# Three modulation blocks move from the first FFN's f tiles into the first mixer of a two-layer trunk

## The chip, the cores and the metric

The kernel runs on one core of one Trainium2 chip. The metric is device time in microseconds (us), the median of several executions. Each profile is of one execution.

## What is computed

The reference is a two-layer decoder trunk over 256 tokens of width 1024, in float32. Every sub-layer normalises, scales and shifts by a vector made from the conditioning row `c`, and adds its gated output:

```python
c_act = silu(c)
for i in range(2):
    mod = c_act @ mod_w[i] + mod_b[i]                 # 9 vectors of 1024
    sh1, sc1, g1, sh2, sc2, g2, sh3, sc3, g3 = split(mod, 9)
    h = rmsnorm(x, norm_g[i, 0]) * (1 + sc1) + sh1
    x = x + 0.5 * g1 * swiglu(h, w13[i, 0], w2[i, 0])          # d_ff 2816
    h = rmsnorm(x, norm_g[i, 1]) * (1 + sc2) + sh2
    x = x + g2 * (pool_ssd_mixer(h) if i == 0 else mla_mixer(h))
    h = rmsnorm(x, norm_g[i, 2]) * (1 + sc3) + sh3
    x = x + 0.5 * g3 * swiglu(h, w13[i, 1], w2[i, 1])
return rmsnorm(x, final_norm_g)
```

## The kernel before

**The weights' stream.** Every weight matrix is cut into blocks of 128 x 2048 float32 (1 MB), and the blocks stand in one hand-written list, `items`. SP issues their transfers in that order into six `raw` buffers. A block of kind "w" is worked off in two halves of eight 128x128 tiles ("pieces"): ScalarE (ACT) copies the half to `wh` (L207), VectorE (DVE) writes what is left to `wl` (L213), and TensorE (PE) multiplies with both, since each product is made of a high and a low part. `take()` hands the pieces to PE and keeps four of them made ahead (`LOOK`); five `wh` and `wl` buffers stand behind that.

**Modulation.** The vectors `mod` are not made on PE. A block of kind "m" holds 256 columns of `mod_w`; each of its two halves is one DVE instruction, which multiplies 128x1024 weights by the broadcast `c_bc` and sums along the row into `modc` (L236), with a short read of the accumulator behind it. It is tied to come after the DVE instruction emitted just before it:

```python
prior = last_vector()
V.scalar_tensor_tensor(out=sl, in0=sl, scalar=1.0, in1=c_bc, op0=ALU.mult,
                       op1=ALU.mult, accum_out=modc[:, c0 : c0 + 1])
tc.add_manual_dep(last_vector(), prior.name, ORDER, reason="program order")
```

**Where the blocks of modulation go.** 64 blocks "m" are dealt out between the weight blocks. `phase(blocks, n_mods, skip)` spreads `n_mods` of them evenly behind the weight blocks of one stage, and `MODS` has the number for each stage, in this order: first FFN w13, first FFN w2 (the f tiles), first mixer input (10 blocks), first mixer output projection (4 of its 6 blocks), second FFN w13 and w2, third FFN w13 and w2, second mixer's input and query stages, last FFN:

```python
for i, (ap, n) in enumerate(blocks):
    items.append(("w", ap, n))
    while mods and done * (len(blocks) - skip) < (i + 1 - skip) * n_mods:
        done += 1
        items.append(mods.pop(0))
```

The order of the vectors is fixed: gate 1, scale 2, shift 2, gate 2, scale 3, shift 3, four blocks each, then those of later sub-layers.

**The stages around the change.** In an FFN, `ffn` makes 22 tiles of a and b, then eight f tiles d = 0 to 7, each of 22 pairs of matmuls (L286 with `wh` on the high and low part of `g`, L287 with `wl`); 11 blocks of w2 carry them. Behind each f tile come two residual updates (`xt`, L466), and the next norm's `chunk` (ACT L395 and squares, DVE L396 and L403). `mixer_ab` opens with tiles named B, C and xs on the un-normalised input (`norm.open`, L280 to L282), then makes z and xs tiles (`lin`), convolutions (L681), the products cb, the pooling input u (in four parts), then eight pairs of heads (`heads`, `ymm`), gates and group norms (L852 to L868), and the output projection o: six tiles are kept open and their k range is cut at 4, 8 and 12 (`CUT_A`, `OPEN_A`), then d = 6 and 7 come whole (`rest`). The next FFN opens behind it with tiles u_a and u_b. The order of instructions on each engine is made by a scheduler from the program order and from what is ready; an engine runs its own instructions in that fixed order.

Of the kernel before, what the change touches and what calls it, by code (L numbers as in the profile page):

```python
# [35 lines left out]
U_DVE = 1  # L36
SKIP = 6
SKIP0 = 3
MODS = (10, 11, 3, 0, 8, 8, 8, 8, 3, 1, 4)
NQ = 3  # L40
CUT_M, OPEN_M = (4, 6, 8), 3

# [19 lines left out]
def trunk(ctx, tc, xT, c_row, colsh, pos, kc, cols, rows, mod_w, w13s, w13c, w13, w2, win_a, wdt,  # L62
# [41 lines left out]
    def phase(blocks, n_mods, skip=0):  # L104
        done = 0
# [6 lines that stand above are left out]
    def ffn_items(i, n13, n2):  # L112
        phase([(w13[i * NJ + j - NS], 16) for j in range(NS if i == 0 else 0, NJ)], n13, SKIP if i else SKIP0)
        phase([(w2[i, j], 16) for j in range(11)], n2)

    ffn_items(0, *MODS[0:2])
    phase([(win_a[b], 16) for b in range(U_END)], MODS[2])
    items.append(("f", pool_w, 13))
    phase([(win_a[b], 16) for b in range(U_END, 12)], 0)
    phase([(wout_a[b], 16) for b in range(1)], 0)  # L120
    phase([(wout_a[b], 16) for b in range(1, 5)], MODS[3])
    phase([(wout_a[5], 16)], 0)
    ffn_items(1, *MODS[4:6])
    ffn_items(2, *MODS[6:8])
    phase([(win_m[b], 16) for b in range(4)], MODS[8])
    phase([(wkv[:, 0 : 16 * P], 16), (wkv[:, 16 * P :], 8)], 0)
# [1249 lines left out]
```

## Time and profile before

| what | value |
|---|---|
| median of 3 runs | 1020.24 us (1019.9 to 1023.21) |
| the profiled execution | 1020.18 us |
| its span, first to last instruction | 1018.4 us |
| PE, DVE, ACT busy | 99%, 87%, 61% |
| bytes read from memory | 252.81 MB, 249 GB/s over the span |

The span is what the rows count from; the 1.8 us around it belong to the launch. A busy PE is not PE at its peak, because matmuls are pipelined, so what tells is where PE is idle and who ended it.

### The profile page before, as it was taken

To read this page: it belongs to the slowest core of one execution; us is meant where nothing else is said; L and a number is where in the kernel's file an instruction comes from. 1 tells how busy PE (TensorE), PEld (TensorE's weight loads), DVE (VectorE), ACT (ScalarE), POOL (GpSimd) and SP (SyncE) were. 2 spreads that over 40 slices of the span, in tenths; PEclk is the share of its full clock that TensorE was granted. 3 is DMA by queue.
4 is the path that set the end of the run, shared out by engine and by line. 5 is a ranking of instruction groups with operands and counts; after the bars stand their busy time and mean duration, and the time that the engine had idled before them with its cause. 6 is when DMAs were issued, how large, how long until landed. Compare 5 with 4: busy or idle time off the path is not lost.

```text
span 1018.4 us, 16658 instructions
## 1 busy us (share of the span) xinstructions
PE 1003.1 (99%) x6300; PEld 891.2 (88%) x6300; DVE 885.9 (87%) x1649; ACT 622.0 (61%) x1141; POOL 0.2 (0%) x4
## 2 busy tenths in 40 slices
PE   9999999999999999999999999999999999999997
PEld 7998888889878988888898888889998898888886
DVE  6999998998999898989979988999998789877663
ACT  4685553458896676555447666555688666666542
POOL 0000000000000000000000000000000000000000
PEclk9999999999999999999999999999999999999999
DMA  9988989976644478889875887898743246766501
GB/s 351 414 340 314 353 311 345 347 268 239 251 166 166 130 254 283 291 292 338 301 261 173 314 294 258 298 339 313 269 162 130 83 166 212 272 223 245 180 28 41
DMA packets 39649, 254.94 MB, mean 250 GB/s; under 512 B 4481, under 2 KB 7057, under 8 KB 10514
## 3 DMA queue, kind: packets, MB, share of 16 engines
q1 hardware_dynamic: 39570, 253.89, 68.9%
q8 instruction: 49, 0.80, 0.3%
q14 instruction: 30, 0.25, 0.1%
HBM read 252.81 MB, written 1.06 MB: 249 GB/s over the span
## 4 chain that ended last, share of the span: by engine, by line
PE 92%; DVE 6%; ACT 1%; issue 0%; DVEq 0%; ACTq 0%
PE f L286 14%; PE a L286 13%; PE b L286 13%; PE f L287 7%; PE a L287 7%; PE b L287 7%; PE n L543 4%; PE o L286 4%; DVE raw L236 2%; DVE wl L213 2%; PE o L287 2%; PE s L1107 1%; PE u_a L281 1%; PE u_a L280 1%; PE u_b L281 1%; PE u_b L280 1%
## 5 line engine op out<-in xcount | busy, mean ns | idle before, releaser
L207 ACT CAST wh<-raw 128x1024 fp32r<-128x1024 f32 x327 | 341.1, 1050 | 239.2 <-PE f L286 69.0
L213 DVE TENSOR_TENSOR wl<-raw,wh 128x1024 fp32r<-128x1024 f32 x327 | 396.6, 1218 | 63.7 <-ACT wh L207 63.1
L286 PE MATMUL f<-g,wh 128*128 128x512 f32 x704 | 244.5, 393 | 0.0
L286 PE MATMUL a<-hx,wh 128*128 128x512 f32 x568 | 201.9, 394 | 0.0
L286 PE MATMUL b<-hx,wh 128*128 128x512 f32 x568 | 201.8, 394 | 0.0
L287 PE MATMUL f<-g,wl 128*128 128x256 f32 x704 | 195.4, 279 | 3.3 <-DVE wl L213 3.3
L236 DVE SCALAR_TENSOR_TENSOR raw<-raw,c_bc 128x1024 f32<-128x1024 f32 x144 | 170.7, 1216 | 0.2 <-DMA raw<-in_mod_w 0.2
L287 PE MATMUL a<-hx,wl 128*128 128x256 f32 x568 | 158.3, 279 | 0.0
L287 PE MATMUL b<-hx,wl 128*128 128x256 f32 x568 | 158.3, 279 | 0.0
L286 PEld LDWEIGHTS f<-g,wh 128*128 128x128 f32 x704 | 131.5, 187 | 29.5
L287 PEld LDWEIGHTS f<-g,wl 128*128 128x128 f32 x704 | 132.5, 188 | 4.9 <-DVE wl L213 4.4
L286 PEld LDWEIGHTS b<-hx,wh 128*128 128x128 f32 x568 | 106.5, 187 | 24.5
L286 PEld LDWEIGHTS a<-hx,wh 128*128 128x128 f32 x568 | 106.5, 187 | 24.5 <-DVE hx L421 0.3
L287 PEld LDWEIGHTS a<-hx,wl 128*128 128x128 f32 x568 | 107.0, 188 | 0.4
L287 PEld LDWEIGHTS b<-hx,wl 128*128 128x128 f32 x568 | 107.0, 188 | 0.4
L334 ACT CAST g<-g 128x256 fp32r<-128x256 f32 x88 | 35.2, 403 | 24.9 <-DVE g L617 18.7
L395 ACT ACTIVATE uh<-xt,gs_t 128x256 fp32r<-128x256 f32 x40 | 20.3, 508 | 44.6 <-DVE xt L466 44.5
L286 PE MATMUL o<-hx,wh 128*128 128x512 f32 x128 | 45.8, 401 | 0.0
L466 DVE SCALAR_TENSOR_TENSOR xt<-f,gt_t,xt 128x256 f32<-128x256 f32 x64 | 30.7, 479 | 15.1 <-PE f L287 14.7
L543 PE MATMUL n<-hx,wh 128*128 128x256 f32 x224 | 40.3, 283 | 0.0
L335 DVE TENSOR_TENSOR g<-g,g 128x256 fp32r<-128x256 f32 x88 | 36.6, 419 | 3.9 <-ACT g L334 3.7
L614 ACT COPY tb<-b 128x256 f32<-128x256 f32 x71 | 26.1, 368 | 18.2 <-PE b L287 18.0
(399 smaller groups left out, 1685.5 us busy)
## 6 DMA issues: line engine op xcount, KB each, us to landing
raw<-in_w SPq DMA_DIRECT2D x124, 1024.0 KB, 4.9
raw<-in_mod_w SPq DMA_DIRECT2D x64, 1024.0 KB, 5.0
raw<-in_win_a SPq DMA_DIRECT2D x12, 1024.0 KB, 5.8
raw<-in_mod_w SPq DMA_DIRECT2D x16, 512.0 KB, 9.4
raw<-in_w13c SPq DMA_DIRECT2D x6, 1024.0 KB, 10.7
raw<-in_wout_a SPq DMA_DIRECT2D x6, 1024.0 KB, 4.7
raw<-in_wq SPq DMA_DIRECT2D x5, 1024.0 KB, 5.1
raw<-in_win_m SPq DMA_DIRECT2D x4, 1024.0 KB, 4.8
```

What stands on the lines that cost most here:

```text
L207: A.copy(wh[:, :n], src)
L213: V.tensor_tensor(out=wl[:, :n], in0=src, in1=wh[:, :n].bitcast(F32), op=ALU.subtract)
L236: V.scalar_tensor_tensor(out=sl, in0=sl, scalar=1.0, in1=c_bc, op0=ALU.mult, op1=ALU.mult, accum_out=modc[:, c0 : c0 + 1])
L280: T.matmul(pt, wl, xh, start=first, stop=False)
L281: T.matmul(pt, wh, xl, start=False, stop=False)
L286: T.matmul(pt, wh, x, start=first, stop=False)
L287: T.matmul(pt[:, S:], wl, x[:, 0], start=False, stop=last)
L334: A.copy(dh, src)
L335: V.tensor_tensor(out=dl, in0=src, in1=dh.bitcast(F32), op=ALU.subtract)
L466: V.scalar_tensor_tensor(out=xt[:, d], in0=pt[:, e * S : (e + 1) * S], scalar=gate[:, d : d + 1], in1=xt[:, d], op0=ALU.mult, op1=ALU.add)
L543: T.matmul(tile_of(m), w_, x[:, k], start=k == 0 and m % 2 == 0 and w_ is w[1], stop=k == NC - 1 and w_ is w[0] and x is hh, skip_group_ch ...
L614: A.copy(p, pt[:, S:])
```

## The change

The number of modulation blocks behind the f tiles of the first FFN goes from 11 to 8, that behind the first mixer's input blocks from 3 to 4, and that in its output projection from 0 to 2.

```diff
-MODS = (10, 11, 3, 0, 8, 8, 8, 8, 3, 1, 4)
+MODS = (10, 8, 4, 2, 8, 8, 8, 8, 3, 1, 4)
```

The total and the order of the blocks stay. By `phase`, the f tiles' blocks of w2 numbered 0 to 10 had a block of modulation behind each, and now have one behind 0, 1, 2, 4, 5, 6, 8 and 9. The mixer's input blocks had one behind 0, 3 and 6, and now have one behind 0, 2, 5 and 7. The output projection now has one behind its blocks 1 and 3.

## Rows read from the trace of the kernel before

**Rows 1.** The profile's page: busy time by engine, and the chain that ended last.

```profile
PE 1003.1 (99%) x6300; PEld 891.2 (88%) x6300; DVE 885.9 (87%) x1649; ACT 622.0 (61%) x1141; POOL 0.2 (0%) x4
...
PE 92%; DVE 6%; ACT 1%; issue 0%; DVEq 0%; ACTq 0%
```

**Rows 2.** Waits of PE: who waited for whom, us in total, times, longest.

```profile
PE f L287 <- DVE wl L213: 3.3, 3, 1.7
PE u_B L281 <- DVE ul L396: 1.6, 1, 1.6
...
PE y L842 <- DVE nw_g L368: 0.9, 1, 0.9
...
PE u_B L280 <- ACT uh L395: 0.3, 1, 0.3
```

**Rows 3.** Busy time by stretch: stretch and length, each engine, PE clock, DMA.

```profile
142.30:176.30 34.00, 34.00 (x195) 29.34 (x193) 30.31 (x52) 15.78 (x23) 0.00 (x0) 1.00 0.87 333
176.30:215.70 39.40, 34.13 (x205) 29.77 (x205) 38.28 (x64) 16.69 (x24) 0.00 (x0) 1.00 0.91 344
215.70:219.20 3.50, 3.50 (x17) 3.32 (x16) 3.04 (x5) 2.30 (x3) 0.00 (x0) 0.51 0.92 321
...
306.50:322.10 15.60, 15.60 (x87) 13.28 (x88) 15.35 (x32) 10.94 (x21) 0.00 (x0) 1.00 0.45 142
322.10:343.50 21.40, 21.40 (x137) 19.23 (x136) 20.14 (x39) 12.65 (x23) 0.00 (x0) 1.00 0.50 180
461.60:524.00 62.40, 62.40 (x366) 54.76 (x365) 57.33 (x93) 32.06 (x43) 0.00 (x0) 1.00 0.89 322
```

**Rows 4.** First f matmul and the norm's sum, first and second FFN (timeline, tile, chain).

```profile
142.31 0.28 PE L287 MATMUL f<-g,wl 128*128 128x256 f32 x1
...
216.33 0.85 PE ss L341 x2
...
L287 PE MATMUL f<-g,wl x168: 274/277/280, 461.9 to 519.8; 128*128 128x256 f32 x168
...
528.58 0.43 PE ss L341 x2
```

**Rows 5.** DVE and PE in order of time, first FFN's f tiles: start, length, [idle before].

```profile
174.53 1.22 DVE L236 SCALAR_TENSOR_TENSOR raw<-raw,c_bc 128x1024 f32<-128x1024 f32 x1
...
175.67 1.22 DVE L236 SCALAR_TENSOR_TENSOR raw<-raw,c_bc 128x1024 f32<-128x1024 f32 x1
...
178.09 0.39 PE L287 MATMUL f<-g,wl 128*128 128x256 f32 x1 [1.73 <-DVE wl L213]
```

**Rows 6.** DVE and PE in order of time, first mixer's input.

```profile
242.32 0.20 DVE L747 COPY acs<-acs 128x48 f32<-128x48 f32 x1
...
247.72 0.48 DVE L681 SCALAR_TENSOR_TENSOR cv<-xraw,colt,cv 128x255 f32<-128x255 f32 x1 [0.98 <-ACT cv L677]
...
258.58 1.22 DVE L236 SCALAR_TENSOR_TENSOR raw<-raw,c_bc 128x1024 f32<-128x1024 f32 x1
...
262.44 2.35 DVE L213 TENSOR_TENSOR wl<-raw,wh 128x1024 fp32r<-128x1024 f32 x2
...
263.80 0.36 PE L280 MATMUL xs<-hx,wl 128*128 128x256 f32 x1
```

**Rows 7.** DVE and PE in order of time, the output projection's first group.

```profile
310.19 0.95 DVE L859 TENSOR_TENSOR gss<-gss,gsq 128x256 f32<-128x256 f32 x2
311.05 1.22 DVE L213 TENSOR_TENSOR wl<-raw,wh 128x1024 fp32r<-128x1024 f32 x1
312.18 1.43 DVE L335 TENSOR_TENSOR hx<-xs,hx 128x256 fp32r<-128x256 f32 x4
...
312.66 0.50 PE L286 MATMUL o<-hx,wh 128*128 128x512 f32 x1
```

**Rows 8.** DVE and PE in order of time, the output projection's end.

```profile
342.64 0.42 DVE L403 TENSOR_TENSOR ss<-ss,sq 128x256 f32<-128x256 f32 x1
...
343.41 0.28 PE L281 MATMUL u_a<-ul,wh 128*128 128x258 f32 x1
```

## The prediction, made before the changed kernel ran

> **What bounds the kernel now.** I read the page first. PE is busy 99% of the span and makes 92% of the chain that ended last, so the kernel is PE's stream of matmuls, and time can be gained only where PE waits or runs slowly [rows 1]. The chain has 6% on DVE; the next view, PE's waits, says where. Of the waits over 0.5 us near the change, one group is on the wl halves of the first FFN's f tiles (3.3 us in three), and two follow at once on the first mixer's opening tiles, 1.6 and 0.3 us. The whole first mixer shows one wait, 0.9 us [rows 2]. Between 176.3 and 215.7 us DVE is busy 38.28 of 39.40 us and PE only 34.13, so here DVE sets the pace. Right behind these waits, at 215.7 us, the granted clock is 0.51 for 3.5 us, that is almost wholly at 1.2 instead of 2.4 GHz [rows 3].
>
> That stage has 11 blocks of modulation among 11 weight blocks. The second FFN does the same f tiles with 8, in just the pattern that the change gives the first, and there PE is busy 62.40 of 62.40 us at full clock, with DVE at 57.33 [rows 3].
>
> **The change, part by part.**
>
> *What leaves the f tiles.* Three blocks are six L236 instructions. Their starts are 1.14 us apart [rows 5], so six are 6.9 us of DVE. The first wait shows the mechanism: the two L236 at 174.53 and 175.67 run ahead of the wl half that PE wants, and PE stands 1.73 us [rows 5]. DVE lacks 5.3 us of PE time there (39.40 less 34.13, [rows 3]) and gets 6.9 us back, which is enough. Gain: 3.3 + 1.6 + 0.3 = 5.2 us of waits [rows 2]. If they go, the slow clock behind them should go too: 3.5 us at half speed is work of 1.75 us, so 1.7 us more. Together 6.9 us. A second way to size it: from the first f matmul to the norm's sum the first FFN takes 74.0 us (142.31 to 216.33), the second 66.7 (461.9 to 528.58), 7.3 us less, to which the slow stretch behind the sum adds up to 1.7 us [rows 3, 4]. The bounds are then 0 (the waits are not DVE's volume but its order) and 9.0. I take 7.0, the nearer to the waits that I can name. The DMA share in the f tiles is 0.87 to 0.91 [rows 3]; three 1 MB transfers fewer can only ease it, and I count nothing for it.
>
> *What comes to the mixer's input.* Two more L236, 2.3 us of DVE, and the others move. That behind input block 3 goes to block 2: DVE does one block in the mixer's opening either way, hidden behind the opening tiles that PE works on without a wait [rows 2], so I count nothing (2.3 us if that cover is gone). The block behind input block 6 ran at 258.58, after the convolution of the fourth xs tile to which it is tied; now one comes behind block 5, tied to the copy at 242.32, and one behind block 7, tied to the cb products, just ahead of the wl pair at 262.44 [rows 6]. The first half of that pair is ready at about 263.66 and PE uses it at 263.80: the reserve is 0.14 us. So 2.3 us more DVE work before it would stop PE for 2.3 less 0.14, unless DVE has idle time to fill. The idle time after the earlier tie is the 0.98 us at 247.72 [rows 6], where DVE waits for ACT and can do the moved block instead. Cost 2.3 - 0.98 - 0.14 = 1.2; with a little for ACT's reply, 1.3 us. Bounds 0 (everything finds idle time) and 2.3. Queued behind the late wl half are the last xs convolutions, and behind these ACT's switch to exponentials for the heads, so a delay here isn't won back later.
>
> *What comes to the output projection.* The first block is emitted right after the last gate product and so tied to the gss sum, which ends at 311.1 us. Behind that sum DVE does one wl half and then the high/low split hx at 312.18, whose first part ends at about 312.5; PE starts on it at 312.66 [rows 7]. There is no reserve. The scheduler prefers what stands earlier in the program, so the two L236 go ahead of the split: 2.3 us later, less 0.2 reserve, is 2.1 us of PE. Only the wl half could be put back, which would halve it. Bounds 0 and 2.3. The second block is tied to a wl half in the pause in which the second group's norm goes round DVE and ACT, and can take the place of wl halves there; they then run in the residual stretch, where DVE is busy 20.14 of 21.40 us [rows 3] and the last sum starts at 342.64, 0.8 us ahead of PE's use of that last chunk at 343.41 [rows 8]. 2.3 less 0.8 less 1.3 idle would be 0.2 us, all of it 2.3; I take 0.8.
>
> The transfers of these blocks are no new cost: they are in the same SP queue, in the same order, only three are issued later, into stretches where the DMA share is 0.45 to 0.50 [rows 3]. What that covers: 3 MB at the f tiles' 344 GB/s would be 8.7 us if nothing hid it. Scale 3 and shift 3 are finished later; they are wanted only at the mixer's end and by the next FFN, and a few small DVE instructions do that, counted at nothing as the residual updates' pauses hide them; without that cover, some 0.5 us.
>
> Sum: 7.0 - 1.3 - 2.1 - 0.8 = 2.8 us less. The profiled execution took 1020.18 us, which is the median of the runs within 0.1, so **1017.4 us**.
>
> [...] The clock fell after the 1.6 us wait at 215 us and not after the 1.73 us wait at 178 us [rows 2, 3, 5], so rows show one fall in two waits of this size. The new waits of 1.3 and 2.1 us in the mixer could each bring one, 1.7 us apiece, or neither. [...]
>
> **The rivals.**
> 1. *The mixer hides all three blocks.* For it: PE waits only 0.9 us in the whole mixer [rows 2]. Against it: reserves of 0.14 and 0.2 us [rows 6, 7]. Then 1020.2 - 7.0 = 1013.2 us.
> 2. *Slower: the output projection becomes what the f tiles were.* From 306.5 to 343.5 us DVE is idle 0.25 + 1.26 = 1.5 us [rows 3], and 4.6 us arrive. If the split and the end each lose a block's 2.3 us and the clock falls behind each, that is 4.6 + 3.4 = 8.0, with 1.3 from the input 9.3 against 7.0: 1022.5 us. It decides from the point where the mixer's loss passes 7.0 us. Against it: wl halves there can wait.
> 3. *The change doesn't do what it says.* The f tiles' waits are a loop: DVE's residual update waits for PE, ACT's copies stand behind it, PE waits for both; less DVE work then frees only half, 3.5 us, and with 4.2 us lost in the mixer it is 1020.9 us. Against it: the second FFN runs the same loop with 8 blocks and no wait [rows 3].
>
> **How the numbers follow.** A measurement of this kernel tells about 0.3% (3.1 us) from no change, so faster means under 1017.1 us and slower over 1023.3. The forecast has 0.50, over 1015.5 to 1019.3, split about evenly by 1017.1; rival 1 has 0.20, rival 2 0.15, rival 3 0.15. Faster: 0.20 + 0.25 = 0.45. Same: 0.25 + 0.12 of rival 3 + 0.07 of rival 2 = 0.44. Slower: 0.08 of rival 2 (with one more fall of the clock, at the input's wait, 1024.2) + 0.03 of rival 3 (with falls of the clock) = 0.11. The range for 8 in 10 reaches to rival 1 below and almost to rival 2 above, 1013.0 to 1022.0, and leaves out about half of each.
>
> **What would show it.** Right: no wait of PE on wl in the first f tiles, clock 1.00 at the mixer's opening, the sum of rows 4 some 7 us earlier; a new wait of PE on wl at the last xs tile of about 1.3 us, and one on hx at the second cut of o of about 2 us, with L236 just ahead of it on DVE. Wrong: waits left in the f tiles, or none in the mixer, or a fall of the clock there.

## The result: slower by 0.6%

The changed kernel took 1028.92 us in the median of 7 runs (1024.78 to 1033.19), the kernel before 1022.72 in 7 runs on the same chip (1019.9 to 1025.2). The ratio is 1.0063 [1.0044, 1.0081], so it is slower by 4.5 to 8.3 us, where 2.8 us less was forecast. The span of the profiled execution went from 1018.4 to 1026.8 us.

The waits of PE in the kernel after (who waited for whom, us in total, times, longest; to be held against [rows 2]):

```profile
PE u_a L280 <- DVE uh L388: 4.8, 1, 4.8
PE o L286 <- DVE hx L335: 2.2, 1, 2.2
...
PE ss L341 <- DVE ul L389: 1.0, 1, 1.0
PE y L842 <- DVE nw_g L368: 0.9, 1, 0.9
...
PE xs L280 <- DVE wl L213: 0.8, 1, 0.8
...
PE xs L280 <- ACT sz L697: 0.3, 1, 0.3
```

The waits on wl in the first f tiles and those at the mixer's opening tiles are gone. The wait on hx at the second cut of o is there as forecast. In the input PE waits 0.3 us at the first of the last four xs tiles (231.29 us) and 0.8 us at the third of them (251.27), and not at the last, where the wait was forecast. New and unforeseen is the first line: the second FFN's first opening tile, u_a, stands 4.8 us for `uh L388`, and 1.0 us follows at once for `ul L389`. These two lines write the shift columns (shift 3): the opening tiles have 258 columns, 256 of tokens and behind them the shift's, and every k step of every opening tile reads its own. `norm.open` calls `shift()` at its beginning, that is in the program behind the whole output projection.

Windows of the kernel after (stretch and length, then PE, PEld, DVE, ACT, POOL, PE clock, DMA share, GB/s, as in [rows 3]):

```profile
176.30:210.00 33.70, 33.69 (x209) 30.00 (x208) 29.99 (x49) 15.60 (x23) 0.00 (x0) 1.00 0.85 322
210.00:213.50 3.50, 3.50 (x30) 3.45 (x29) 3.50 (x7) 2.16 (x3) 0.00 (x0) 1.00 0.94 309
309.00:334.40 25.40, 25.40 (x143) 22.03 (x144) 24.68 (x49) 14.30 (x25) 0.00 (x0) 1.00 0.65 244
334.40:339.40 5.00, 0.30 (x2) 0.00 (x0) 5.00 (x12) 2.04 (x4) 0.00 (x0) 1.00 0.79 234
339.40:346.20 6.80, 5.71 (x23) 5.29 (x24) 2.90 (x7) 0.94 (x3) 0.00 (x0) 0.50 0.34 140
```

The f tiles end with PE busy 33.69 of 33.70 us, and the mixer opens at full clock. The loss stands in the last two lines: 5.0 us in which PE has two matmuls and DVE is busy all the time, and then 6.8 us at a granted clock of 0.50, that is at 1.2 GHz. PE is busy 5.71 us of that stretch. A matmul of the opening lasts 0.55 us there and 0.28 us at full clock, so at full clock the same work would take half, and the clock is worth 2.9 us.

PE's first matmul of the opening, in the kernel before and in the one after (start, length, engine, line, operation, tiles, [idle before]):

```profile
338.25 0.28 PE L280 MATMUL u_a<-uh,wl 128*128 128x258 f32 x1
```

```profile
339.52 0.55 PE L280 MATMUL u_a<-uh,wl 128*128 128x258 f32 x1 [4.83 <-DVE uh L388]
```

What DVE did meanwhile, in order of time, kernel after:

```profile
315.59 1.22 DVE L236 SCALAR_TENSOR_TENSOR raw<-raw,c_bc 128x1024 f32<-128x1024 f32 x1
316.74 0.08 DVE L236 DVE_READ_ACCUMULATOR raw<-raw,c_bc 128x1 f32 x1
...
327.68 0.48 DVE L396 SCALAR_TENSOR_TENSOR ul<-xt,gs_t,uh 128x256 fp32r<-128x256 f32 x1 [0.72 <-ACT uh L395]
...
335.98 0.87 DVE L466 SCALAR_TENSOR_TENSOR xt<-o,gt_t,xt 128x256 f32<-128x256 f32 x2
336.77 0.15 DVE L313 TENSOR_TENSOR sh_t<-modc,colt 128x8 f32<-128x8 f32 x1
336.84 1.22 DVE L213 TENSOR_TENSOR wl<-raw,wh 128x1024 fp32r<-128x1024 f32 x1
337.98 0.48 DVE L396 SCALAR_TENSOR_TENSOR ul<-xt,gs_t,uh 128x256 fp32r<-128x256 f32 x1
338.37 0.42 DVE L403 TENSOR_TENSOR ss<-ss,sq 128x256 f32<-128x256 f32 x1
338.71 0.48 DVE L466 SCALAR_TENSOR_TENSOR xt<-o,gt_t,xt 128x256 f32<-128x256 f32 x1
339.10 0.16 DVE L388 CAST uh<-sh_t 128x8 fp32r<-128x8 f32 x1
339.17 1.22 DVE L213 TENSOR_TENSOR wl<-raw,wh 128x1024 fp32r<-128x1024 f32 x1
...
341.04 0.17 DVE L389 TENSOR_TENSOR ul<-sh_t,uh 128x8 fp32r<-128x8 f32 x1
```

The last sum of shift 3 is complete at 316.82 us. The three instructions that make columns of it last 0.15 to 0.17 us each, and start 20, 22 and 24 us later, with other work between them. In the kernel before, whose program has them in the same place, they were done 58 us ahead of u_a (kernel before, DVE in order of time, [idle before]):

```profile
278.87 0.16 DVE L313 TENSOR_TENSOR sh_t<-modc,colt 128x8 f32<-128x8 f32 x1
279.60 0.56 DVE L834 TENSOR_TENSOR lm<-lm,cbm 128x384 f32<-128x384 f32 x1 [0.57 <-ACT lm L833]
280.08 0.17 DVE L388 CAST uh<-sh_t 128x8 fp32r<-128x8 f32 x1
280.28 0.18 DVE L389 TENSOR_TENSOR ul<-sh_t,uh 128x8 fp32r<-128x8 f32 x1
```

There the sums were complete before the heads, and DVE, waiting for ACT between the heads, had room for what stood far behind in the program. After the change they are complete only in the output projection, where DVE is busy 24.68 of 25.40 us and then 5.00 of 5.00. Its one pause there, 0.72 us ahead of 327.68, was not used for them. The order on DVE is fixed before the program runs, and why the scheduler set it so is not shown by a trace; what the place costs is shown by runs 1 and 2.

Where the time came from and went can be summed from the starts of the same matmul in both traces. Each is set against the first f matmul, which starts 0.37 us later after the change:

| matmul | before | after | gained (−) or lost so far | of it new |
|---|---|---|---|---|
| first f | 142.31 | 142.68 | 0 | |
| first z tile, behind the openings | 232.37 | 224.69 | −8.05 | −8.05 f tiles and clock |
| last xs tile | 263.80 | 257.79 | −6.4 | +1.7 input |
| o, second cut | 312.99 | 309.33 | −4.0 | +2.3 first output block |
| second FFN's u_a | 338.25 | 339.52 | +0.9 | +4.9 columns and second block |
| second FFN's first a, behind the openings | 356.23 | 361.32 | +4.7 | +3.8 second wait, half clock |

So the change cost 4.7 us by place in this profile, inside the interval of the ratio. The span differs by 8.4 us: 0.4 lay ahead of the first f, and some 3 us come between the first a of the second FFN and one a matmul well inside the third, the same in both traces (229.0 us before, 232.1 after), without a wait in the list or a lower clock. That part is taken up at the end.

### The profile page after: what moved, and what is told of

The parts are those of the page before. It is cut to its first block, busy times and chain, and to the rows that moved or that the text cites. A ratio compares the mean times of both kernels' runs of the same rounds, so it can differ in the third digit from the quotient of the medians.

```text
span 1026.8 us, 16661 instructions
## 1 busy us (share of the span) xinstructions
PE 1007.6 (98%) x6300; PEld 893.7 (87%) x6300; DVE 885.5 (86%) x1649; ACT 622.2 (61%) x1141; POOL 0.2 (0%) x4
## 4 chain that ended last, share of the span: by engine, by line
PE 92%; DVE 5%; ACT 3%; issue 0%; DVEq 0%; ACTq 0%
PE f L286 16%; PE a L286 13%; PE b L286 13%; PE f L287 8%; PE a L287 7%; PE b L287 7%; PE n L543 4%; PE o L286 3%; DVE wl L213 1%; PE o L287 1%; PE s L1107 1%; DVE cv L681 1%; PE u_a L281 1%; PE u_a L282 1%; PE u_a L280 1%; PE u_b L281 1%
## 5 line engine op out<-in xcount | busy, mean ns | idle before, releaser
L286 PE MATMUL f<-g,wh 128*128 128x512 f32 x704 | 245.6, 395 | 0.0
L286 PE MATMUL a<-hx,wh 128*128 128x512 f32 x568 | 202.6, 396 | 0.0
L286 PE MATMUL b<-hx,wh 128*128 128x512 f32 x568 | 202.5, 395 | 0.0
L287 PE MATMUL f<-g,wl 128*128 128x256 f32 x704 | 196.0, 279 | 0.0
L236 DVE SCALAR_TENSOR_TENSOR raw<-raw,c_bc 128x1024 f32<-128x1024 f32 x144 | 170.8, 1215 | 0.1
L287 PE MATMUL a<-hx,wl 128*128 128x256 f32 x568 | 158.8, 280 | 0.0
L287 PE MATMUL b<-hx,wl 128*128 128x256 f32 x568 | 158.8, 280 | 0.0
L286 PEld LDWEIGHTS f<-g,wh 128*128 128x128 f32 x704 | 131.8, 188 | 30.6
L287 PEld LDWEIGHTS f<-g,wl 128*128 128x128 f32 x704 | 132.6, 188 | 0.3
L286 PEld LDWEIGHTS a<-hx,wh 128*128 128x128 f32 x568 | 106.5, 188 | 25.2 <-DVE hx L421 0.4
L286 PEld LDWEIGHTS b<-hx,wh 128*128 128x128 f32 x568 | 106.5, 188 | 25.0
L287 PEld LDWEIGHTS b<-hx,wl 128*128 128x128 f32 x568 | 107.1, 189 | 0.3
L287 PEld LDWEIGHTS a<-hx,wl 128*128 128x128 f32 x568 | 107.1, 189 | 0.3
L286 PE MATMUL o<-hx,wh 128*128 128x512 f32 x128 | 46.0, 402 | 2.2 <-DVE hx L335 2.2
```

Source lines behind the costliest of these rows:

```text
L286: T.matmul(pt, wh, x, start=first, stop=False)
L287: T.matmul(pt[:, S:], wl, x[:, 0], start=False, stop=last)
```

## The experiments

Two theories stood against each other. **A**: the loss is the place of the three small instructions; the columns come late, PE waits, the clock falls. **B**: it is the volume that the prediction's second rival named; 4.6 us of L236 are too much for DVE in the output projection, and the columns only show where it ends.

**1. The columns asked for earlier in the program.** In the changed kernel, `shift()` is called between the second and the last cut. It does the same work.

```diff
         proj.cut(1)
+        nxt.shift()
         proj.cut(2)
         proj.rest()
```

> The changed kernel with one line more: the three small DVE instructions that put shift 3 into its columns (L313, L388, L389) are emitted behind the second cut of o, so that they come before the residual updates. Same blocks in the same places. Theory A (the columns come late because the last quarter of shift 3 is now made in the output projection, and PE's opening tiles read them): the 4.8 and 1.0 us waits at u_a and the half clock behind them (6.8 us, worth 3.4) go, about 9 us less than the changed kernel, that is about 3 us less than the kernel before (ratio 0.997). Rival B (the two blocks' 4.6 us of DVE work make the whole residual chain late, and the columns only show it): PE then waits 3 to 5 us at the opening for the last residual chunk instead, and the time stays within 3 us of the changed kernel (ratio 1.003 to 1.006).

Measured: 1018.51 us (12 runs), ratio to the kernel before 0.9980 [0.9963, 0.9997]. DVE in order of time in this run, and below it the waits of PE:

```profile
318.31 0.16 DVE L313 TENSOR_TENSOR sh_t<-modc,colt 128x8 f32<-128x8 f32 x1
...
319.52 0.17 DVE L388 CAST uh<-sh_t 128x8 fp32r<-128x8 f32 x1
...
319.99 0.16 DVE L389 TENSOR_TENSOR ul<-sh_t,uh 128x8 fp32r<-128x8 f32 x1
```

```profile
PE o L286 <- DVE hx L335: 2.2, 1, 2.2
...
PE xs L280 <- DVE wl L213: 0.8, 1, 0.8
...
PE u_a L281 <- DVE ul L396: 0.5, 1, 0.5
```

With the same blocks in the same places, the three instructions start 2.4, 3.6 and 4.1 us after the last sum is complete (315.91 us), the wait on L388 is gone, the clock stays at 1.00, and what is left of the end's wait is 0.5 us. From u_a to the first a it takes 18.94 us (333.63 to 352.57), against 17.98 in the kernel before: by place, the second block still costs 1.0. A holds, and B falls: the volume is unchanged. (Both blocks in the output projection belong to shift 3, so it is the second half of shift 3 that is made there, not the last quarter.)

**2. Only the columns late.** In the kernel before, the first instruction of `shift()` for the second FFN is tied behind the DVE instruction emitted before it, that is behind the last sum of squares (L403), which follows the last residual update. No block moves.

```diff
+            late = last_vector()
             self.sh = prep_shift(*self.ls)
+            if self.ls == (0, 2):
+                tc.add_manual_dep(last_vector(), late.name, ORDER, reason="program order")
```

> The kernel before, no block moved; only the three small instructions of shift 3 are tied behind the last residual chunk, which is where the program emits them. Theory A: PE's opening tiles, due at 338 us, wait till the columns are written at about 343 us, and the clock falls behind that: 5 us plus up to 3.4, so 7 to 9 us slower (ratio 1.007 to 1.009). Rival B (volume of DVE work): nothing was added, 0 to 1 us slower.

Measured: 1028.91 us (6 runs), ratio 1.0088 [1.0064, 1.0111]. Waits of PE and windows of this run (its lines are numbered 3 higher from L387 on, so its L392 is L389):

```profile
PE u_a L280 <- DVE ul L392: 5.2, 1, 5.2
PE f L287 <- DVE wl L213: 3.3, 3, 1.7
```

```profile
334.00:342.80 8.80, 4.68 (x27) 3.79 (x25) 8.30 (x15) 4.48 (x9) 0.00 (x0) 1.00 0.51 159
342.80:349.60 6.80, 5.74 (x27) 5.77 (x28) 0.94 (x5) 0.00 (x0) 0.00 (x0) 0.50 0.25 106
```

The wait and the slow stretch come without any moved block; the second FFN's first a starts at 364.43 instead of 356.23 us, 7.8 later when both are set against the first f as in the table. So late columns alone cost 7.8 us by place, and by the ratio 6.5 to 11.3 us.

**3. All three blocks to the input** (the output projection as before). It separates what a block costs in the one place and in the other.

```diff
-MODS = (10, 8, 4, 2, 8, 8, 8, 8, 3, 1, 4)
+MODS = (10, 8, 6, 0, 8, 8, 8, 8, 3, 1, 4)
```

> Counts 10, 8, 6, 0: all three blocks go to the mixer's input, none to its output projection. The f tiles' gain of 7 us stays. Theory A: shift 3 is ready before the heads, so no wait at u_a; the input pays for three blocks instead of one, 1.3 plus two times 2.3 less what idle time of DVE takes up, so 2 to 6 us: 1 to 5 us faster than before (ratio 0.995 to 0.999). Rival B (the mixer as a whole has no room on DVE, wherever the blocks go): all 6.9 us of DVE work come back as waits, time as before or slower (ratio 1.000 to 1.003).

Measured: 1021.70 us (12 runs), ratio 1.0016 [0.9996, 1.0035]: no change that can be told. The waits of PE in it:

```profile
PE xs L280 <- DVE cv L681: 1.7, 1, 1.7
PE y L842 <- DVE lm L834: 1.2, 1, 1.2
...
PE z L280 <- ACT hx L420: 0.8, 1, 0.8
...
PE xs L280 <- DVE wl L213: 0.7, 1, 0.7
```

The first z tile starts 7.9 us earlier than before, but the first o only 1.8: the input gives back 6.1 us for three more blocks, 2.0 each, against 1.7 for the single one of the change. There is little cover in the input. No wait on the columns, and no fall of the clock. The time is not what A expected (0.995 to 0.999): it lies in the range that this run's rival B gave. By place 1.9 us are still gained at the second FFN's first a; in this profile the matmuls of the last FFN then run at the slower of the two paces that the last section describes, so the time alone does not settle what the three blocks are worth in the input.

**4. Two blocks in the output projection that nobody waits for.** As 3, with two blocks of gate 3 taken from the second FFN into the output projection; shift 3 is complete in the input. B expects the loss here, A doesn't.

```diff
-MODS = (10, 8, 4, 2, 8, 8, 8, 8, 3, 1, 4)
+MODS = (10, 8, 6, 2, 6, 8, 8, 8, 3, 1, 4)
```

> Counts 10, 8, 6, 2, 6: as the run with all three in the input, but two blocks of gate 3, which is wanted only in the next FFN's f tiles, stand in the output projection, and the next FFN has two fewer. The same 4.6 us of DVE work in the same places as in the changed kernel, without the hurry. Theory A: about 2 us over the all-input run, for the split hx behind the first block, and no wait at u_a. Rival B: the wait at u_a comes back with the work, 6 to 9 us over the all-input run.

Measured: 1022.01 us (12 runs), ratio 1.0025 [1.0008, 1.0042]. The two lines that are new in the waits of PE against run 3 and matter here:

```profile
PE o L286 <- DVE hx L335: 2.0, 1, 2.0
...
PE u_a L281 <- DVE ul L396: 0.5, 1, 0.5
```

The second FFN's u_a starts at 338.76 against 336.42 in run 3, 2.1 us later when both are set against the first f, nearly all of it at the split for the second cut; its first a starts 3.0 us later, with the wait on ul. So two blocks of volume cost 3.0 us by place, near the 2.1 + 0.8 of the prediction, and the clock doesn't fall. The 6 to 9 us that B expected do not come.

**5. Also the first output block later.** As 1, with the two blocks of the output projection behind its blocks 3 and 4 and not 1 and 3, and `shift()` behind the last cut.

```diff
-    phase([(wout_a[b], 16) for b in range(1)], 0)
-    phase([(wout_a[b], 16) for b in range(1, 5)], MODS[3])
+    phase([(wout_a[b], 16) for b in range(3)], 0)
+    phase([(wout_a[b], 16) for b in range(3, 5)], MODS[3])
...
         proj.cut(2)
+        nxt.shift()
         proj.rest()
```

> The changed kernel with the output projection's two blocks behind its blocks 3 and 4 instead of 1 and 3, and the columns of shift 3 emitted behind the third cut of o. Theory A (the 2.2 us wait at o is the first block standing ahead of the split hx, and the late columns are the rest of the loss): neither the wait at o nor that at u_a is left; 2 us under the run with the columns early, about 5 us under the kernel before (ratio 0.995). Rival B (DVE's volume in the output projection): the work moves on into the residual updates and PE waits 2 to 4 us at the opening for the last chunk, so no better than the run with the columns early (ratio 0.998 or more).

Measured: 1017.37 us (12 runs), ratio 0.9960 [0.9945, 0.9975]: faster than both kernels, 2.6 to 5.6 us under the one before. The waits of PE at the place:

```profile
PE u_b L280 <- DVE ul L389: 0.7, 1, 0.7
PE u_a L280 <- DVE uh L388: 0.6, 1, 0.6
PE u_a L281 <- DVE ul L396: 0.5, 1, 0.5
```

The wait on hx is gone, since L236 no longer stands ahead of the split; three small ones take its place at the end, two of them on the columns, which are late again. The second FFN's u_a starts at 332.68 us, 5.6 earlier than before, but its first a only 3.7. Run 1 comes to 3.2 there: of the 2 us that this run was expected to gain over run 1, 0.5 is seen by place, and the intervals of the two ratios overlap. So what is taken away at the split comes back for the most part at the opening, as this run's rival B had it, if by less than its 2 to 4 us.

**6. The pause filled.** The changed kernel with 12 more matmuls between the output projection and the opening, on old data into an unused tile; what the kernel computes stays the same. It asks what of the loss is the wait and what the clock.

```diff
         proj.rest()
+        wm = ps("fill")
+        for _ in range(12):
+            T.matmul(wm[:, :S], onesf, xt[:, 5], start=True, stop=True)
```

> The changed kernel with twelve matmuls of ones against a part of x (into an unused PSUM tile, about 0.43 us each) between the last o tile and the next FFN's opening, so that PE isn't idle while it waits for the columns; the columns stay late. Theory A (a wait of 4.8 us and then 6.8 us at half clock, of which the second is worth 3.4 us): the clock stays at 1.00 and the time is 3 to 4 us under the changed kernel (ratio 1.002 to 1.004). Rival C (the half clock costs nothing, since DVE and ACT are late there anyway): the time is that of the changed kernel (ratio 1.006).

Measured: 1026.15 us (12 runs), ratio 1.0045 [1.0025, 1.0065], against 1.0063 [1.0044, 1.0081] without them. The intervals overlap, so by time alone it is inconclusive, and the 3 to 4 us that were expected are not there. PE in order of time, and windows:

```profile
333.88 5.34 PE L922 MATMUL fill<-xt,onesf 128*128 128x256 f32 x24
338.88 0.47 PE L280 MATMUL u_a<-uh,wl 128*128 128x258 f32 x1
...
340.62 0.67 PE L341 MATMUL ss<-ss,onesf 128*128 128x256 f32 x2 [1.15 <-DVE ul L389]
```

```profile
334.20:341.00 6.80, 5.65 (x29) 4.85 (x27) 6.36 (x14) 2.49 (x5) 0.00 (x0) 1.00 0.84 284
341.00:346.00 5.00, 5.00 (x43) 4.97 (x42) 1.10 (x3) 0.31 (x1) 0.00 (x0) 1.00 0.08 34
```

Here the rows decide: u_a starts 0.64 us earlier than in the changed kernel, which is what the first f does too (142.05 against 142.68), but the clock stays at 1.00. From u_a to the first a it takes 19.57 us (338.88 to 358.45) and in the changed kernel 21.80 (339.52 to 361.32), 2.2 us less. The half clock follows from the pause in PE's work and not from the late columns in another way. Of the 2.9 us that the clock was put at, 0.2 is taken by the wait on L389 (1.15 us here, 0.97 there), and 0.5 stays open.

**7. The input's block alone.** One block from the f tiles to the input, none to the output projection.

```diff
-MODS = (10, 8, 4, 2, 8, 8, 8, 8, 3, 1, 4)
+MODS = (10, 10, 4, 0, 8, 8, 8, 8, 3, 1, 4)
```

> Counts 10, 10, 4, 0: one block from the f tiles to the mixer's input, the rest as before. Theory A, from the terms measured so far: the f tiles get back 2.3 us of DVE of the 5.2 us of waits, and perhaps the slow clock behind them (1.7); the input gives up 1.3 to 1.7: between 2.5 us faster and equal (ratio 0.9975 to 1.000). Rival D (the f tiles' waits and clock go only when nearly all surplus is gone): no gain there, 1 to 2 us slower (ratio 1.001 to 1.002).

Measured: 1020.47 us (12 runs), ratio 0.9981 [0.9961, 1.0000]. The first z tile starts at 228.36, 4.0 us earlier than before, the last xs tile 2.4. The wait of PE on wl in the f tiles is untouched:

```profile
PE f L287 <- DVE wl L213: 3.3, 3, 1.7
```

What is gone is the 1.6 us wait on the opening and the slow stretch behind it. So the first block that leaves buys the opening and the clock, and the waits on wl inside the f tiles need the other two. The input's block costs 1.6 us here.

**8. Run 1 once more**, one profile only.

> The same kernel as the first run, for its profile alone. In that run's profile pairs of matmuls in the second FFN stood 353 ns apart, where the kernel before has 347 at the same granted clock. If the pace belongs to the kernel, it is 353 again; if it belongs to the execution, it may be 347, and the span some 4 us shorter.

Measured: 1017.42 us. Its span is 1015.4 us, and that of run 1's profile 1020.6: 5.2 us between two executions of one kernel. The twelve executions of run 1 itself, all on one chip, lie as far apart, from 1016.76 to 1022.62 us. The first a matmul of the second FFN and one a matmul well inside the third (the same in both), of run 1 and then of run 8, in order of time:

```profile
352.57 0.28 PE L287 MATMUL a<-hx,wl 128*128 128x256 f32 x1
...
585.18 0.28 PE L287 MATMUL a<-hx,wl 128*128 128x256 f32 x1
```

```profile
353.27 0.28 PE L287 MATMUL a<-hx,wl 128*128 128x256 f32 x1
...
582.30 0.28 PE L287 MATMUL a<-hx,wl 128*128 128x256 f32 x1
```

The same stretch takes 232.6 and 229.0 us. The changed kernel's profile had 232.1 in it and that of the kernel before 229.0. A difference of this size in this stretch is therefore no evidence of a change.

## Why the prediction was wrong, step by step

- **The f tiles** (forecast 7.0 us gained): right. 8.05 us by place; the named waits and the slow clock were 6.9, and the second estimate by the second FFN, up to 9.0, held the value; where the other 1.1 came from is not traced. The step from one wait's mechanism to DVE's volume was sound: PE is busy 33.69 of 33.70 us in the tiles' second part.
- **The mixer's input** (1.3 lost): right in stage and size, not in the tile. 1.7 us by place, with waits of 0.8 and 0.3 us, but at the third and first of the last four xs tiles. At the last, where the sum had put the wait, PE doesn't wait. The reserve ahead of it stayed at about 0.1 us (wl ends at about 257.6, PE uses it at 257.79).
- **The first output block** (2.1 lost): right. Two L236 at 305.09 and 306.24 stand ahead of the split, and PE waits 2.19 us for it. Run 5 shows it from the other side: with the block elsewhere, the wait is gone.
- **The second output block** (0.8 lost): right in kind. With the columns mended, 0.5 us of wait on ul is left (runs 1 and 4), 1.0 us by place.
- **The step that failed**: "Scale 3 and shift 3 are finished later; they are wanted only at the mixer's end and by the next FFN, and a few small DVE instructions do that, counted at nothing as the residual updates' pauses hide them; without that cover, some 0.5 us." Neither the value nor the bound held. The cost of these instructions isn't their 0.5 us of DVE but where they stand in its queue. They came 20 to 24 us after their data, PE stood 4.83 and 0.97 us for them, and the clock was low from the end of the first wait on, worth 2.9. That is 8.7 us, and by place, too, the end lost 4.9 + 3.8 = 8.7, where 0.8 was forecast. Of this 1.0 is the second block, which is left in run 1, and 7.8 the columns. Runs 1 and 2 show it both ways: mended alone, the change comes to 0.9980 [0.9963, 0.9997], near the 2.8 us of the sum (0.9973), and to 3.2 us less by place; made alone, the late columns cost 7.8 us by place. The pauses that were to hide these instructions are the 1.26 us of idle time of [rows 3], which the sum had already set against the second block.
- **The number**: the forecast of 1017.4 us started from 1020.18 us, and the median of 7 runs of the kernel before is 1022.72. So 2.5 of the 11.5 us between forecast and result are the start, and 9.0 the change: 6.2 lost where 2.8 were to be gained.
- **The rivals**: the second one named the right stage and a fall of the clock at its end, but by a wrong mechanism: two blocks' volume costs 3.0 us there (run 4), not 4.6, and brings no fall of the clock. The first (the mixer hides all) and the third (the f tiles give only half) are refuted by 4.0 us of input and first block and by 8.05 us.
- **The clock**: the rows had one fall in two waits. After the change it fell at 339.38 us, as the wait of 4.83 us ended and ahead of that of 0.97 us. It didn't fall after that of 2.2 us, and in runs 1 and 4 after none. The prediction weighed a fall for the two waits that it foresaw, and the wait that brought one was not among them. The Trainium skill ("TensorE: Matmul & The Clock Gate", "Why this matters for your kernels") asks that PE have no long idle gaps between bursts of matmuls, since the clock goes back to half after one. The falls at the waits of 4.83 us and, in run 2, of 5.18 us agree with that; the fall after 1.6 us in the kernel before shows that a shorter wait can bring one too.

## What to carry to other kernels

When work is moved to a later stage, follow its result to every reader, the smallest too: an instruction of 0.16 us whose result the next stage's opening matmuls read is on the path as soon as its data come late. Cost it by its place in its engine's order (what is emitted before it, and what else the engine has to do between data and reader), and not by its length; ask for it in the program as soon as its data are there. With that, the same three blocks out of the f tiles make the kernel 0.2% (run 1) or 0.4% (run 5) faster than before. Whether it pays to set the blocks behind the split, too, as run 5 does, is not shown: by place it gives 0.5 us.

## What the runs showed of the hardware beyond that

- The granted clock of TensorE fell to 0.50 for 3.41 us after a wait of 1.6 us in the kernel before (at 215.75 us) and in run 2 (at 216.46). It fell for 6.83 us in the kernel after at 339.38, where a wait of 4.83 us ended, and in run 2 at 342.76, within one of 5.18 us. It didn't fall after 1.73 us (kernel before, 178 us) or 2.2 us (at the second cut of o). With 24 matmul passes put into the 4.8 us pause it stayed at 1.00. The length of the wait alone doesn't order these cases.
- At a granted clock of 1.00 and without waits, the pair of matmuls L286 and L287 comes every 346.7 or every 353.4 ns for whole stages (mean from start to start of successive L287 in the order of time). It was the slower value in the second FFN of the changed kernel's execution and in the second and third FFN of run 1's, and the faster in both of run 8's, whose kernel is run 1's. In the stretch that run 8 compares it comes to 3.6 us, where the verdicts here turn on 2 to 9. In the executions of runs 3, 6 and 7 the last FFN has the slower value. The cause stays open.
